# Summing the second MLP product over groups in DRAM instead of in on-chip tiles

## The chip, the cores and the metric

The kernel runs on one core of a Trainium2 chip. The metric is the time of one execution on the device in microseconds (us). Before the change three runs gave 1573.42, 1578.68 and 1580.87 us, so the median is 1578.68 us. One execution was recorded by the hardware profiler; its time and its trace are described below.

## What is computed

The reference is a two-layer block on 512 tokens of x and 256 tokens of a context, with 1024 features. Both streams share all weights. Each layer does, in this order:

- a modulated RMS norm, then a projection `zx = hx @ w_in`;
- token mixers on the projected features: an mLSTM in both directions, a Fourier mixer and a depthwise convolution, joined by `@ w_out`;
- a residual step with a norm and a gate;
- a second modulated norm, then the MLP, again followed by a norm, a gate and a residual step.

In layer 1 the context's output is not needed, so only the 512 tokens of x go through the projections after the keys and values. The part that the change touches is the MLP:

```
def sq_relu_mlp(h, w1, w2):
    return jnp.square(jax.nn.relu(h @ w1)) @ w2

hx = modulate(rmsnorm(x, g_pre_mlp[l]), mx[3], mx[4])
x = x + mx[5] * rmsnorm(sq_relu_mlp(hx, w_mlp1[l], w_mlp2[l]), g_post_mlp[l])
```

`w_mlp1` is 1024 x 4096 and `w_mlp2` is 4096 x 1024. All values are 32-bit floats.

## The kernel before

**Tiles.** Tokens are cut into six blocks of 128 (two of context, four of x). Every matrix is split into a high part and a low part, and a product is three matmuls: high times high, high times low and low times high. A weight tile is loaded as raw 32-bit numbers by a DMA that SP issues (L213), ScalarE (ACT) copies it to the high part (L219), and VectorE (DVE) subtracts to get the low part (L220). The function `prep` does this, `weight` hands out a finished pair, and calls `prep` for weights up to two ahead in a fixed list called `stream`.

**The MLP.** The 4096 hidden features are taken in eight groups `g` of 512, each of four tiles `f` of 128. For a group the first product gives the squared hidden values `gt[f]` (a high and a low tile each), and the second product, `mlp2` (L1025), multiplies them with the group's four weight tiles. Group 0 uses the plain first product. Groups 1 to 7 use `mlp1_pair`, a generator that makes two hidden tiles with seven half-size products (L1094) instead of eight; a group runs two such generators, `one_` and `two_`, interleaved by `next` calls. Between their steps stand calls of `background()`, which in layer 0 also work on the modulation of layer 1 (loads at L338, DVE products at L342).

In `mlp1_pair` the products of a late stage are accumulated on top of a PSUM bank `X` that ACT has to copy out first (L1118, L1124), so TensorE (PE) waits for that copy.

**The second product before.** For each half `hf` of the 1024 output columns and each block `b`, twelve matmuls fill one PSUM bank. In group 0 ACT copies the bank to the tile `acc[b]`, in groups 1 to 6 DVE adds it to `acc[b]`, and in group 7 it is added and the post-norm, gate and residual follow:

```
if g == 0:
    S.activation(ac_, ps, AF.Copy)
else:
    V.tensor_tensor(ac_, ps, ac_, ALU.add)
```

**Buffers.** `t4` is a pool of 8 tiles of 128 x 1024, `raw` one of 3 such tiles, `whi` has 6 and `wlo` 5 slots for the split weights, `mm` and `aux` are 4 PSUM banks each. In layer 0 the six `acc` tiles and, as long as the modulation of layer 1 runs, two more tiles (`box["c"]`) fill all of `t4`; in layer 1 it is four `acc` tiles. The raw weights of the MLP, the other weights and the background's loads share the three `raw` slots.

**What sets the order.** The instructions are written in program order, and a planner then lays out one fixed order for each engine from modelled durations: at every point it takes the ready instruction that stands first in program order, so a matmul of a later step may go ahead of an earlier one that is planned to wait. Slots of a pool are given out in program order. On the chip each engine and each DMA queue then keeps its order, and an instruction at its head that waits holds up what stands behind it.

Of the kernel before, what the change touches and what calls it, by code (L numbers as in the profile page):

```python
# [10 lines left out]
F32 = mybir.dt.float32  # L11
F32R = mybir.dt.float32r
AF = mybir.ActivationFunctionType
# [51 lines left out]
def build(tc, a):  # L65
# [20 lines left out]
    def nm(s):  # L86
        n_names[0] += 1
        return f"{s}{n_names[0]}"
# [59 lines left out]
    xd = [drp.tile([128, D], F32, name=f"xd{b}") for b in range(NB)]  # L148
    gd = [[drp.tile([2, D], F32, name=f"gd{l}_{g}") for g in range(2)] for l in range(DEPTH)]
    cd = drp.tile([2, D], F32, name="cd")  # L150
    md = [drp.tile([8, TOK], F32, name=f"md{l}") for l in range(DEPTH)]


# [31 lines left out]
    def prep(n):  # L185
        while st["next"] < min(n, len(stream)):
            key, src, (p, q) = stream[st["next"]]
            st["next"] += 1
            hi = hip.tile([128, 1024], F32R, tag="hi", name=nm("hi"))
            lo = lop.tile([128, 1024], F32R, tag="lo", name=nm("lo"))  # L190
            n_ = p * q
            parts = [t[:, :n_].rearrange("p (k n) -> p k n", k=p) for t in (hi, lo)]
            ready[key] = parts
            if key[0] == "dft":
                for i in range(2):
                    P.dma_start(parts[i], src[i])
                continue
            r0, n0 = 0, n_
            if key[0] in ("wt1", "wt2"):
                r1, r2 = pairs[key[1:]]  # L200
                if key[0] == "wt1":
                    raw = r2
                    V.tensor_tensor(r2[:, 0:512], r2[:, 0:512], r1[:, 0:512], ALU.subtract)
                    V.tensor_tensor(r2[:, 512:1024], r2[:, 512:1024], r2[:, 0:512], ALU.subtract)
                else:
                    raw = r1
                    V.tensor_tensor(r1.rearrange("p (k n) -> p k n", k=2), r1.rearrange("p (k n) -> p k n", k=2),
                                    r2[:, 512:1024].unsqueeze(1).to_broadcast([128, 2, 512]), ALU.subtract)
            elif key in pre:
                raw = pre.pop(key)  # L210
            else:
                raw = rawp.tile([128, 1024], F32, tag="raw", name=nm("raw"))
                dma(raw[:, :n_].rearrange("p (k n) -> p k n", k=p), src)  # L213
                if key[0] in ("wb1", "wb2"):
                    pairs.setdefault(key[1:], []).append(raw)
                    if key[0] == "wb2":

                        r0 = 512
            S.activation(hi[:, r0:n0], raw[:, r0:n0], AF.Copy)  # L219
            V.tensor_tensor(lo[:, r0:n0], raw[:, r0:n0], hi[:, r0:n0].bitcast(F32), ALU.subtract)  # L220
# [247 lines left out]
    def layer(l, res, nbg, first=None):  # L468
# [539 lines left out]
        yield "normed", None  # L1008


        acc = {}

        def mlp1_out(o, t0, n, th, tl):
            r = c2()
            S.activation(r[:, :n], o[:, :n], AF.Relu)
            V.tensor_tensor(r[:, :n], r[:, :n], r[:, :n], ALU.mult)
            split(r[:, :n], th[:, t0:t0 + n], tl[:, t0:t0 + n], True)

        def mlp2(ps, b, gt, ws, c0=0, c1=512):
            n = 0  # L1020
            for f in range(4):
                hi, lo = ws[f // 2]
                th, tl = gt[f]
                for hp, wp in ((th, hi), (th, lo), (tl, hi)):
                    T.matmul(ps, hp[:, 128 * b:128 * b + 128], wp[:, f % 2, c0:c1], start=n == 0, stop=n == 11)  # L1025
                    n += 1

# [106 lines left out]
        between = []  # L1136
        for g in range(NF // 4):
            gt = [(t3(F32R), t3(F32R)) for f in range(4)]
            if g == 0:

                w1 = [weight("w1", l, f) for f in range(4)]
# [7 lines left out]
            else:  # L1149
# [7 lines left out]
                background()  # L1157
                next(two_)
                background()
                for _ in two_:  # L1160
                    pass
                background()
            if g < NF // 4 - 1:
                for hf in range(2):
                    ws = [weight("w2", l, 4 * g + 2 * hf + i) for i in range(2)]
                    for b in oblk:
                        if b not in acc:
                            acc[b] = t4()
                        ps = mm()
                        mlp2(ps, b, gt, ws)  # L1170
                        ac_ = acc[b][:, 512 * hf:512 * hf + 512]
                        if g == 0:
                            S.activation(ac_, ps, AF.Copy)
                            if between:
                                between.pop(0)()
                        else:
                            V.tensor_tensor(ac_, ps, ac_, ALU.add)  # L1177
                continue
            G = {v: gate_row(l, 1, v) for v in ((0,) if last else (1, 0))}
            ws = [[weight("w2", l, 4 * g + 2 * hf + i) for i in range(2)] for hf in range(2)]  # L1180
            for b in oblk:
                o = acc[b]
                xr = [t3(), t3()]
                for hf in range(2):
                    dma(xr[hf][:, :512], xd[b][:, 512 * hf:512 * hf + 512])
# [1 line left out]
                cuts = (0, 256, 512, 768, 1024) if last and b == NB - 1 else (0, 512, 1024)  # L1187
                ms = None
                for i, (c0, c1) in enumerate(zip(cuts, cuts[1:])):
                    ps = mm()[:, :c1 - c0]  # L1190
                    h0 = 512 * (c0 // 512)
                    mlp2(ps, b, gt, ws[c0 // 512], c0 - h0, c1 - h0)
                    ac_ = o[:, c0:c1]
                    V.tensor_tensor(ac_, ps, ac_, ALU.add)
                    ss = ty(1, f"fs{i}")
# [213 lines left out]
```

## Time and profile before

| | |
|---|---|
| median of 3 runs | 1578.68 us (1573.42 to 1580.87) |
| the profiled execution | 1575.05 us, its span 1573.0 us |
| instructions | 23268 |
| PE busy | 1502.8 us (96%), mean granted clock 0.991 |
| DVE, ACT, POOL busy | 1094.1, 755.6 and 95.8 us |
| DMA | 197.30 MB, mean 125 GB/s |
| MLP of layer 0, groups 1 to 7 | 474.2 to about 942 us of the span |
| MLP of layer 1, groups 1 to 7 | 1255.2 to about 1565 us of the span |

The span runs from the first to the last instruction; the execution's time is 2.05 us longer. POOL is GpSimd, PE is TensorE, PEld its weight loads, SP the engine whose queue issues most DMAs. A clock of 1.00 is the higher of TensorE's two levels, 2.4 GHz, and 0.5 is the lower one, 1.2 GHz. A bracket behind a row gives the time in which the engine did nothing just before it, and what ended that wait.

### The profile page before, as it was taken

The numbers are of one execution on the slowest core, as the hardware profiler recorded it, in microseconds if no ns is written. First come the engines' busy times: TensorE is split into PE (matmuls) and PEld (weight loads), VectorE is DVE, ScalarE is ACT, GpSimd is POOL, SyncE is SP. The second block draws the span as 40 slices with busy tenths as digits, with TensorE's granted clock in tenths as the row PEclk, the third lists the DMA queues.
The fourth block names the chain that finished last, engine by engine and source line by source line (L and its number), as shares of the span: only waits on it lengthen the run. The fifth ranks groups of instructions, "written<-read, shape, count | busy, mean of one in ns | idle before, by whom it ended". The sixth has DMA issues, their size and how long they took to land. (4 is left out here: it accounts for less than half of the span.)

```text
span 1573.0 us, 23268 instructions
## 1 busy us (share of the span) xinstructions
PE 1502.8 (96%) x8926; PEld 1308.6 (83%) x8926; DVE 1094.1 (70%) x2101; ACT 755.6 (48%) x1471; POOL 95.8 (6%) x233
## 2 busy tenths in 40 slices
PE   7889999999998999999999998999999999999997
PEld 5868888987888889797888978788888888888886
DVE  3449987855899776675755575799756976666665
ACT  4633244536645343342524575544437655555443
POOL 0001022101000000000000011111101000000000
PEclk9999999999999999999999999999999999999999
DMA  8545436523534352441523332322225133333223
GB/s 322 136 140 191 158 109 209 194 73 134 181 102 137 105 188 89 139 151 64 187 68 107 103 134 101 122 80 80 83 81 174 55 120 98 104 108 96 94 81 119
DMA packets 65582, 197.30 MB, mean 125 GB/s; under 512 B 11904, under 2 KB 14368, under 8 KB 65472
## 3 DMA queue, kind: packets, MB, share of 16 engines
q1 hardware_dynamic: 64032, 191.10, 36.5%
q0 software_dynamic: 1440, 4.72, 0.9%
q8 instruction: 70, 1.15, 0.3%
q14 instruction: 40, 0.33, 0.1%
HBM read 183.13 MB, written 12.66 MB: 124 GB/s over the span
## 5 line engine op out<-in xcount | busy, mean ns | idle before, releaser
L219 ACT ACTIVATE hi<-raw 128x1024 fp32r<-128x1024 f32 (+1 forms) x245 | 244.6, 999 | 400.4 <-PE mm L1025 172.1
L1025 PE MATMUL mm<-hi,t 128*128 128x512 f32 (+1 forms) x1296 | 409.8, 394 | 6.8 <-ACT t L230 6.0
L220 DVE TENSOR_TENSOR lo<-raw,hi 128x1024 fp32r<-128x1024 f32 (+1 forms) x245 | 280.7, 1148 | 72.6 <-ACT hi L219 27.7
L1025 PEld LDWEIGHTS mm<-hi,t 128*128 128x128 f32 x1296 | 242.8, 189 | 65.7 <-ACT t L230 10.1
L1025 PE MATMUL mm<-lo,t 128*128 128x512 f32 (+1 forms) x648 | 253.5, 392 | 0.0
L457 PE MATMUL mm<-hhi,hi 128*128 128x256 f32 (+1 forms) x576 | 168.5, 336 | 0.0
L457 PE MATMUL mm<-hhi,lo 128*128 128x256 f32 (+1 forms) x576 | 166.5, 334 | 0.0
L457 PE MATMUL mm<-hlo,hi 128*128 128x256 f32 (+1 forms) x576 | 165.6, 332 | 0.0
L1177 DVE TENSOR_TENSOR t<-mm,t 128x512 f32<-128x512 f32 x120 | 82.3, 689 | 112.8 <-PE mm L1025 112.8
L1094 PE MATMUL mm<-hhi,hi 128*128 128x384 f32 (+1 forms) x448 | 141.0, 315 | 17.7 <-ACT c L1124 10.8
L1025 PEld LDWEIGHTS mm<-lo,t 128*128 128x128 f32 x648 | 122.5, 189 | 25.9
L1094 PE MATMUL mm<-hhi,lo 128*128 128x384 f32 (+1 forms) x448 | 139.1, 311 | 2.3 <-DVE lo L220 2.3
L1094 PE MATMUL mm<-hlo,hi 128*128 128x384 f32 (+1 forms) x448 | 139.0, 310 | 0.0
L457 PEld LDWEIGHTS mm<-hhi,hi 128*128 128x128 f32 x576 | 107.6, 189 | 15.5 <-issue 3.3
L457 PEld LDWEIGHTS mm<-hhi,lo 128*128 128x128 f32 x576 | 108.7, 189 | 12.1 <-issue 1.2
L457 PEld LDWEIGHTS mm<-hlo,hi 128*128 128x128 f32 x576 | 108.4, 189 | 10.9
L1094 PEld LDWEIGHTS mm<-hhi,hi 128*128 128x128 f32 x448 | 84.9, 190 | 25.3 <-ACT c L1124 15.7
L652 DVE SCALAR_TENSOR_TENSOR t<-t,half,t 128x783 f32<-128x783 f32 (+1 forms) x120 | 102.2, 888 | 0.3
L1094 PE MATMUL aux<-t,hi 128*128 128x384 f32 (+1 forms) x448 | 98.6, 310 | 0.2 <-DVE c L1125 0.2
L1094 PEld LDWEIGHTS mm<-hhi,lo 128*128 128x128 f32 x448 | 85.1, 190 | 2.6 <-DVE lo L220 2.6
L1094 PEld LDWEIGHTS mm<-hlo,hi 128*128 128x128 f32 x448 | 85.0, 190 | 0.7
L233 DVE TENSOR_TENSOR t<-c,t 128x256 fp32r<-128x256 f32 (+1 forms) x132 | 62.8, 478 | 24.6 <-ACT t L230 24.1
(244 smaller groups left out, 2729.8 us busy)
## 6 DMA issues: line engine op xcount, KB each, us to landing
raw<-w SPq DMA_DIRECT2D x128, 512.0 KB, 3.6
raw<-w_at SPq DMA_DIRECT2D x48, 512.0 KB, 3.5
raw<-w_a SPq DMA_DIRECT2D x44, 512.0 KB, 4.2
raw<-w_c SPq DMA_DIRECT2D x32, 512.0 KB, 5.1
xd<-t SPq DMA_DIRECT2D x20, 512.0 KB, 2.8
raw<-w_o SPq DMA_DIRECT2D x16, 512.0 KB, 3.6
t<-xd SPq DMA_DIRECT2D x20, 256.0 KB, 5.8
t<-x SPq DMA_DIRECT2D x8, 512.0 KB, 6.0
```

Source lines behind the costliest of these rows:

```text
L219: S.activation(hi[:, r0:n0], raw[:, r0:n0], AF.Copy)
L220: V.tensor_tensor(lo[:, r0:n0], raw[:, r0:n0], hi[:, r0:n0].bitcast(F32), ALU.subtract)
L233: V.tensor_tensor(blk_lo, src, blk_hi.bitcast(F32), ALU.subtract)
L457: T.matmul(o[:, :n], wp[:, k, :], hp[:, k, t0:t0 + n], start=k == 0 and i == 0, stop=k == KB - 1 and i == 2)
L652: V.scalar_tensor_tensor(o, u[j][:, o0 + k:o1 + k], w, o, ALU.mult, ALU.add)
L1025: T.matmul(ps, hp[:, 128 * b:128 * b + 128], wp[:, f % 2, c0:c1], start=n == 0, stop=n == 11)
L1094: T.matmul(ps[:, :HN], wp[:, K2 * j + k, :], hp, start=first and k == 0 and i == 0, stop=k == K2 - 1 and i == 2, skip_group_check=True)
L1177: V.tensor_tensor(ac_, ps, ac_, ALU.add)
```

## The change

Three things are changed together.

1. The tiles `acc` go. In groups 0 to 6 ACT copies each PSUM bank to a fresh `t4` tile. In group 0 a DMA of SP's queue writes it to a new DRAM tensor `ad[l][b]`; in groups 1 to 6 a DMA of POOL's queue adds it to what is there (`accum_op=ALU.add`). In group 7 the sum is loaded back to a `t4` tile and the rest goes on as before.
2. The raw weights of the MLP (`w1`, `w2`, `wb1`, `wb2`) are loaded to tiles of `t4` instead of `raw`.
3. In groups 1 to 7 the first two weight tiles of the second product are fetched before the last step of `two_`, and the matmuls of the first two blocks with `f` 0 and 1 are written there, into two PSUM banks that are finished later with `f` 2 and 3.

The diff, cut to its core:

```diff
+    ad = [[drp.tile([128, D], F32, name=f"ad{l}_{b}") for b in range(NB)] for l in range(DEPTH)]
 ...
-                raw = rawp.tile([128, 1024], F32, tag="raw", name=nm("raw"))
+                mlp = key[0] in ("wb1", "wb2", "w1", "w2")
+                raw = t4() if mlp else rawp.tile([128, 1024], F32, tag="raw", name=nm("raw"))
 ...
-        def mlp2(ps, b, gt, ws, c0=0, c1=512):
-            n = 0
-            for f in range(4):
+        def mlp2(ps, b, gt, ws, c0=0, c1=512, fs=range(4)):
+            for f in fs:
                 hi, lo = ws[f // 2]
                 th, tl = gt[f]
-                for hp, wp in ((th, hi), (th, lo), (tl, hi)):
-                    T.matmul(ps, hp[:, 128 * b:128 * b + 128], wp[:, f % 2, c0:c1], start=n == 0, stop=n == 11)
-                    n += 1
+                for n, (hp, wp) in enumerate(((th, hi), (th, lo), (tl, hi))):
+                    T.matmul(ps, hp[:, 128 * b:128 * b + 128], wp[:, f % 2, c0:c1], start=f == 0 and n == 0,
+                             stop=f == 3 and n == 2)
 ...
                 next(two_)
                 background()
+                ws0 = [weight("w2", l, 4 * g + i) for i in range(2)]
+                for b in oblk[:2]:
+                    early[b] = mm()
+                    mlp2(early[b], b, gt, ws0, fs=(0, 1))
                 for _ in two_:
                     pass
 ...
                     for b in oblk:
-                        if b not in acc:
-                            acc[b] = t4()
-                        ps = mm()
-                        mlp2(ps, b, gt, ws)
-                        ac_ = acc[b][:, 512 * hf:512 * hf + 512]
+                        if hf == 0 and b in early:
+                            ps = early[b]
+                            mlp2(ps, b, gt, ws, fs=(2, 3))
+                        else:
+                            ps = mm()
+                            mlp2(ps, b, gt, ws)
+                        o = t4()[:, 0:512]
+                        S.activation(o, ps, AF.Copy)
+                        to = ad[l][b][:, 512 * hf:512 * hf + 512]
                         if g == 0:
-                            S.activation(ac_, ps, AF.Copy)
+                            dma(to, o)
 ...
                         else:
-                            V.tensor_tensor(ac_, ps, ac_, ALU.add)
+                            P.dma_start(to, o, accum_op=ALU.add)
 ...
-                o = acc[b]
+                o = t4()
+                dma(o, ad[l][b])
```

## Rows read from the trace of the kernel before

**Rows 1.** Page, part 1: busy us, share of the span and instructions of each engine.

```profile
PE 1502.8 (96%) x8926; PEld 1308.6 (83%) x8926; DVE 1094.1 (70%) x2101; ACT 755.6 (48%) x1471; POOL 95.8 (6%) x233
```

**Rows 2.** Windows, layer 0's MLP groups: stretch, length, busy per engine, PEclk, DMA share, GB/s.

```profile
542.90:609.80 66.90, 64.80 (x313) 57.49 (x312) 43.80 (x81) 26.13 (x42) 0.00 (x0) 0.97 0.39 127
...
676.50:743.10 66.60, 64.49 (x314) 57.21 (x313) 42.99 (x76) 25.86 (x42) 0.00 (x0) 0.97 0.37 119
...
810.20:874.10 63.90, 63.49 (x315) 56.02 (x314) 37.99 (x62) 25.91 (x42) 0.00 (x0) 1.00 0.31 100
...
sum 424.90, PE 408.57 PEld 363.74 DVE 284.71 ACT 175.36 POOL 0.00; mean PE 58.37 PEld 51.96 DVE 40.67 ACT 25.05 POOL 0.00
```

**Rows 3.** Windows, layer 1's seven MLP groups up to 1542.9 us: their sum.

```profile
sum 287.70, PE 276.88 PEld 247.82 DVE 191.59 ACT 151.25 POOL 0.00; mean PE 39.55 PEld 35.40 DVE 27.37 ACT 21.61 POOL 0.00
```

**Rows 4.** Waits, layer 0's MLP (474 to 905): total us, times, longest us.

```profile
PE mm L1094 <- ACT c L1118: 6.9, 4, 2.0
PE mm L1025 <- ACT t L230: 6.0, 4, 2.1
PE mm L1094 <- DVE lo L220: 2.4, 2, 2.3
...
ACT hi L219 <- DMA raw<-w: 22.3, 20, 3.9
```

**Rows 5.** Waits of PE, ACT and SP's queue, layer 1's MLP (1255 to 1545).

```profile
PE mm L1094 <- ACT c L1124: 10.8, 7, 2.0
...
ACT hi L219 <- DMA raw<-w: 10.2, 11, 1.6
...
SPq L213 <- DVE lo L220: 246.6, 49, 13.0
```

**Rows 6.** Timeline, layer 1, group 1 before `two_`'s last step: start, us, engine, instruction.

```profile
1272.54 0.40 PE L1025 MATMUL mm<-hi,t 128*128 128x512 f32 x1
...
1273.80 1.06 ACT L219 ACTIVATE hi<-raw 128x1024 fp32r<-128x1024 f32 x1 [1.19 <-DMA raw<-w]
...
1275.18 0.40 PE L1094 MATMUL mm<-hhi,hi 128*128 128x256 f32 x1 [1.32 <-ACT c L1124]
```

**Rows 7.** Timeline, layer 0, group 3 after `two_`'s last step.

```profile
642.17 1.06 ACT L219 ACTIVATE hi<-raw 128x1024 fp32r<-128x1024 f32 x1 [1.05 <-DMA raw<-w]
...
648.12 0.50 PE L1025 MATMUL mm<-hi,t 128*128 128x512 f32 x1 [2.10 <-ACT t L230]
```

**Rows 8.** Groups of instructions: count, busy us, mean ns, idle before.

```profile
L1177 DVE TENSOR_TENSOR t<-mm,t 128x512 f32<-128x512 f32 x120 | 82.3, 689 | 112.8 <-PE mm L1025 112.8
...
L1173 ACT ACTIVATE t<-mm 128x512 f32<-128x512 f32 x20 | 11.7, 587 | 3.1 <-PE mm L1025 3.0
```

**Rows 9.** Timeline, DVE, one addition between two blocks of the second product.

```profile
721.14 0.69 DVE L1177 TENSOR_TENSOR t<-mm,t 128x512 f32<-128x512 f32 x1 [2.08 <-PE mm L1025]
```

**Rows 10.** POOL's table loads: duration ns min/median/max, and time to landing.

```profile
L196 POOL DMA_DIRECT2D hi<-dft_x x4: 546/570/595, 255.7 to 1102.6; - x4
...
DMA to landing us min/median/max: 3.6/5.2/8.3
```

**Rows 11.** DMA issues: queue, count, KB each, median us to landing.

```profile
raw<-w SPq DMA_DIRECT2D x128, 512.0 KB, 3.6
...
out<-t SPq DMA_DIRECT2D x8, 256.0 KB, 2.0
```

**Rows 12.** Windows, ten us in which only the second product runs, layer 0.

```profile
584.00:594.00 10.00, 10.00 (x45) 8.11 (x44) 4.97 (x8) 0.70 (x1) 0.00 (x0) 1.00 0.02 10
```

**Rows 13.** Timeline, end of layer 0's last group: ACT, PE, POOL.

```profile
918.23 1.06 ACT L402 ACTIVATE t<-t 128x1024 f32<-128x1024 f32 x1 [0.43 <-DVE t L1198]
...
922.06 1.09 PE L417 MATMUL aux<-ident_sb,t 128*128 128x128 f32 x8 [1.20 <-ACT t L404]
...
944.89 0.55 POOL L396 TENSOR_TENSOR fr<-fs1m,nhalf 128x1 f32<-128x1 f32 x1 [3.75 <-ACT fs1m L391]
...
957.31 2.64 POOL L396 TENSOR_TENSOR pr<-prm,nhalf 128x1 f32<-128x1 f32 x1 [3.48 <-ACT prm L391]
```

More of the change, by code (lines that the diff above doesn't have):

```diff
@@ L1008, in layer @@
         yield "normed", None
-        acc = {}
         def mlp1_out(o, t0, n, th, tl):
@@ L1138, in layer @@
             gt = [(t3(F32R), t3(F32R)) for f in range(4)]
+            ws0, early = None, {}
             if g == 0:
@@ L1164, in layer @@
                 for hf in range(2):
-                    ws = [weight("w2", l, 4 * g + 2 * hf + i) for i in range(2)]
+                    ws = ws0 if ws0 and hf == 0 else [weight("w2", l, 4 * g + 2 * hf + i) for i in range(2)]
                     for b in oblk:
-                        if b not in acc:
-                            acc[b] = t4()
-                        ps = mm()
-                        mlp2(ps, b, gt, ws)
-                        ac_ = acc[b][:, 512 * hf:512 * hf + 512]
+                        if hf == 0 and b in early:
[7 more added lines that the diff above has]
+                        to = ad[l][b][:, 512 * hf:512 * hf + 512]
                         if g == 0:
-                            S.activation(ac_, ps, AF.Copy)
+                            dma(to, o)
                             if between:
@@ L1176, in layer @@
                         else:
-                            V.tensor_tensor(ac_, ps, ac_, ALU.add)
+                            P.dma_start(to, o, accum_op=ALU.add)
                 continue
             G = {v: gate_row(l, 1, v) for v in ((0,) if last else (1, 0))}
-            ws = [[weight("w2", l, 4 * g + 2 * hf + i) for i in range(2)] for hf in range(2)]
+            ws = [ws0] + [[weight("w2", l, 4 * g + 2 + i) for i in range(2)]]
             for b in oblk:
-                o = acc[b]
+                o = t4()
+                dma(o, ad[l][b])
                 xr = [t3(), t3()]
@@ L1189, in layer @@
                 for i, (c0, c1) in enumerate(zip(cuts, cuts[1:])):
-                    ps = mm()[:, :c1 - c0]
                     h0 = 512 * (c0 // 512)
-                    mlp2(ps, b, gt, ws[c0 // 512], c0 - h0, c1 - h0)
+                    if c0 == 0 and b in early:
+                        ps = early[b][:, :c1 - c0]
+                        mlp2(ps, b, gt, ws[0], c0 - h0, c1 - h0, (2, 3))
+                    else:
+                        ps = mm()[:, :c1 - c0]
+                        mlp2(ps, b, gt, ws[c0 // 512], c0 - h0, c1 - h0)
                     ac_ = o[:, c0:c1]
```

## The prediction

> **What bounds the kernel now.** I read the busy times first. TensorE is busy for 1502.8 of 1573.0 us [rows 1], the other engines for 70% or less. So time can only be won where PE stands still or runs slowly, and no part of this change takes a matmul away. Next I cut the MLP into its groups. In layer 0, groups 1 to 7 take 424.9 us to the end of their first products and PE is busy for 408.57 of them: 16.3 us are idle [rows 2]. In layer 1 it is 287.7 against 276.88: 10.8 us idle [rows 3]. Group 6 of layer 0, nearly without idle time, takes 63.9 us with 63.49 of PE; groups 2 and 4 show 64.80 and 64.49 of PE at a mean granted clock of 0.97 [rows 2], so two short falls to the lower level cost 1.3 and 1.0 us, 2.3 together. These 29.4 us are all that the MLP's middle can give back.
>
> Then I asked the waits what stands behind the idle time. In layer 1 it is one thing, seven times: the last step of the second generator waits for ACT's copy L1124, 10.8 us in all [rows 5]. The timeline shows why. PE has run six matmuls of the second product (1272.54 + 6 x 0.23 = 1273.9) and stops until 1275.18. ACT's copy is late because the weight copy L219 in front of it stood 1.19 us for a raw load [rows 6]. The load is late because its issue waits for a `raw` slot: SP's queue waits 246.6 us, 49 times, for the subtraction L220 that frees one [rows 5], while a load lands 3.6 us after its issue [rows 11]. In layer 0 the idle time is mixed: 6.9 us for L1118, 6.0 us for the split of the hidden values L230, 2.4 us for L220 [rows 4]. ACT waits there for raw loads too, 22.3 us, 20 times [rows 4], and of the 2.10 us that PE lost at 648.12 a wait of 1.05 us for a load is directly ahead [rows 7]; the rest is work of ACT and of the background.
>
> **The change part by part.**
>
> Raw weights in `t4`: in layer 1 eight slots instead of three take the raw tiles and the partial sums, in layer 0 six (two hold the background's tiles), and the background has the three `raw` slots to itself. A load then leaves SP some microseconds earlier, and the waits of 1.0 to 1.6 us that delay L1124 go. No instruction is added.
>
> First blocks early: no matmul is added, twelve matmuls of 0.231 us are written before the last step of `two_`, 2.77 us. The planner already moves six of them there in layer 1 [rows 6]; six more are 1.39 us of cover against gaps of 1.3 to 2.0 us. Both edits work on the same seven gaps. I take 9.5 of the 10.8 us as gone; bounds 0 (the planner shifts the wait) and 10.8. In layer 0 I take half of the 16.3 us, 8, because about half of the idle time that I followed has a load ahead of it; bounds 0 and 16.3. Of the clock's 2.3 us I take half, 1.2, as the falls lie beside gaps; bounds 0 and 2.3.
>
> What is late next: after the last step the first blocks need `f` 3, whose values are made last. PE covered that with matmuls of which six more are now spent: at most 1.39 us per group, 13 groups, 18 us. The other two PSUM banks allow two further blocks with three of four `f`, 2 x 9 x 0.231 = 4.2 us of other cover, so I take a loss of 2; bounds 0 and 18.
>
> Sums in DRAM: DVE loses 120 additions of 0.689 us, 82 us; ACT gets 120 copies of 0.587 us, 70 us [rows 8]. A block takes 0.69 + 2.08 = 2.77 us of PE [rows 9], so one copy per block fits. ACT, now busy for 175 of 425 us and 151 of 288 us [rows 2, 3], comes to 217 (72 x 0.587 more) and 179: not a bound. DVE's relief buys nothing by itself, it isn't the bound. Cost 0; if ACT's order puts a copy behind a late load, PE has three further PSUM banks, 8.3 us, before it feels it. POOL issues 120 accumulating DMAs. POOL's issue of a table load takes 0.57 us [rows 10]: 68 us in stretches where POOL is at 0.00 [rows 2, 3], and nothing else is queued behind on POOL until the next norm's power. The trace has no accumulating DMA. Its landing time lies between 2.0 us (a plain 256 KB store, [rows 11]) and, going by twice the slowest load of POOL's queue for reading and writing, 16.6 us (2 x 8.3, [rows 10]). I take 5.2, the median of that queue, the nearest row. A slot of `t4` is then held for 0.59 + 0.57 + 5.2 = 6.4 us, 2.3 blocks, and the slots last. DMA engines have room: in the middle of the second product they are at 0.02 of their time [rows 12].
>
> The Trainium skill ("SBUF — State Buffer", the note on the trap "DVE blocks DMA") says that descriptors of a DMA issued by GpSimd are written by GpSimd itself, which is locked out while VectorE runs an operation that takes the port pair they share. The trace shows a stretch of that kind for POOL's arithmetic, 2.64 us where another takes 0.55, beside a busy DVE [rows 13]; it shows none for a DMA issue, 0.546 to 0.595 us [rows 10]. By the rule the slot life grows by some 2.1 us, to 8.5, which leaves the sum as it is and makes rival C below likelier.
>
> Group 0 and group 7: 20 stores and 10 loads on SP's queue, each needed long after its issue: 0, at worst a late load of 3.6 us at a layer's end. In layer 0's last group the six `acc` and two gate tiles filled `t4`, so the first block's norm could only start when block 1 had freed a gate tile (it waits for L1198 at 918.23), and PE idled 1.20 us at 922.06 [rows 13]. That wait goes: 1.2 (0 to 1.2).
>
> **Sum:** 9.5 + 8 + 1.2 + 1.2 - 2 = 17.9 us. The profiled execution took 1575.05 us, 2.05 more than its span; less 17.9 that is 1557. The median of the runs, 1578.68, is 3.6 above it, so I predict 1561 for the median.
>
> **The rivals.**
>
> *A, the forecast*, 1561: chance 0.58.
>
> *B, the gap only moves.* The six further matmuls are missing behind the last step, where the hidden values' chain through ACT and DVE sets the pace. For it: in layer 0 this is already the place of 6.0 us [rows 4]. Against: more PSUM banks' worth of other matmuls. Price: up to 18 us back, so 1578.7 - 19.9 + 18 = about 1577. Chance 0.20, no change that can be measured (this kernel's runs tell 0.5%, 7.9 us, from nothing).
>
> *C, the accumulating DMA holds the tiles.* In layer 0 six slots serve sums and weights; if weights hold two, four blocks, 4 x 2.77 = 11.1 us, is the longest life of a sum's slot. It decides from a landing of 11.1 - 1.16 = 9.9 us on. Then ACT's copy waits for a slot, with the weight copies behind it, and PE runs out of PSUM. At a landing of 12 us a block takes (12 + 1.16) / 4 = 3.29 us, 0.52 more, times 72 blocks: 37 us lost in layer 0, while layer 1 with six slots (2.19 per block) keeps its gain of 9.5. That is 1578.7 + 37 - 9.5 = 1606. For it: no row shows such a DMA and 8.3 us has occurred. Against: a median of 5.2, and idle DMA engines. Chance 0.16. (By the Trainium skill's rule above the point falls to 7.8 us, below the slowest row, and C would get 0.22.)
>
> *D, everything goes.* All 29.4 and 1.2, no loss: 1578.7 - 30.6 = 1548. Chance 0.06.
>
> **How the numbers follow.** Faster by over 0.5%, below 1570.8, are A and D: 0.64. Within 0.5% is B: 0.20. Slower is C: 0.16. The range reaches down to D with 2 us for the scatter of the runs, 1546, and up into C's milder part, 1590 (a landing of about 11 us); about 0.04 lies below and 0.12 above. A's own range is 1552 to 1570.
>
> **What would show it.** Right: in layer 1 the seven waits for L1124 are gone or below 0.3 us each; ACT's waits for raw loads in the MLP fall from 32 us to under 10; PE idle in the MLP's middle falls from 27 to about 10 us; the accumulating DMAs land in 4 to 7 us; the wait of PE for L230 does not exceed 8 us. B: that wait grows to 20 us or more. C: ACT's copies wait for a DMA of the partial sums, and PE for ACT's copies, in layer 0 above all. Also wrong would be a gain that shows outside the MLP.

## The result and the profile after

The changed kernel takes 1592.04 us (median of six runs, 1589.42 to 1598.54) against 1579.75 us for the kernel before in the same comparison: ratio 1.0088, 95% interval 1.0063 to 1.0114. It is slower by about 0.9%; the forecast was 1561 us. The profiled execution took 1592.11 us with a span of 1590.4 us, 17.4 us more than before.

The page of the changed kernel, parts 1, 3, 5 and 6 (an issue row is: queue, count, KB each, median us to landing):

```profile
PE 1507.0 (95%) x8926; PEld 1312.4 (83%) x8926; DVE 1011.6 (64%) x1981; ACT 818.8 (51%) x1591; POOL 194.7 (12%) x353
...
q1 hardware_dynamic: 68352, 201.59, 37.0%
q0 software_dynamic: 18720, 36.18, 14.0%
...
L1187 POOL DMA_DIRECT2D ad<-t x120 | 103.4, 899 | 680.2 <-ACT t L1180 680.0
...
t<-w SPq DMA_DIRECT2D x128, 512.0 KB, 5.3
ad<-t POOLq DMA_DIRECT2D x120, 256.0 KB, 5.6
raw<-w_at SPq DMA_DIRECT2D x48, 512.0 KB, 4.5
```

With as many matmuls as in [rows 1] PE is busy for 4 us more, at a mean granted clock of 0.982 against 0.991, and stands still for 13 us more. DVE lost the 82 us of its additions, ACT gained 63 where 70 were worked out. Raw weights of the MLP now land 5.3 us after their issue instead of 3.6 [rows 11].

Line numbers have moved by three up to the MLP: L213, L219, L220, L230, L338 and L342 of the kernel before are L216, L222, L223, L233, L341 and L345 here. L1180 is ACT's copy of a partial sum, L1187 POOL's accumulating DMA, L1209 DVE's addition in group 7.

Windows, layer 0's groups 1 to 4 of the changed kernel and the sum of groups 1 to 6 (columns as in [rows 2]):

```profile
480.90:548.60 67.70, 64.85 (x313) 57.13 (x311) 51.79 (x118) 32.63 (x53) 6.99 (x8) 0.97 0.65 190
548.60:627.00 78.40, 65.54 (x313) 58.21 (x313) 54.90 (x138) 30.56 (x53) 11.27 (x13) 0.93 0.84 254
627.00:701.60 74.60, 65.73 (x314) 58.40 (x313) 35.37 (x59) 35.39 (x58) 12.03 (x14) 0.93 0.63 155
701.60:764.50 62.90, 62.90 (x315) 56.12 (x314) 25.49 (x33) 32.41 (x54) 10.28 (x12) 1.00 0.52 115
...
sum 409.20, PE 384.62 PEld 342.07 DVE 218.36 ACT 195.80 POOL 61.19; mean PE 64.10 PEld 57.01 DVE 36.39 ACT 32.63 POOL 10.20
```

Groups 4 to 6 run without a gap, in 62.9 us, which no group of [rows 2] does. Groups 2 and 3 take 78.4 and 74.6, with 13 and 9 us of idle PE and a granted clock of 0.93. What differs between them is DVE's work: 55 and 35 us where groups 4 to 6 have 25. The surplus is the background, the modulation of layer 1.

Layer 1's groups 1 to 6 (the sum in [rows 3] is over seven groups):

```profile
1284.10:1326.60 42.50, 42.48 (x266) 37.64 (x266) 26.85 (x37) 27.95 (x53) 6.11 (x7) 1.00 0.62 166
...
sum 255.30, PE 255.22 PEld 225.39 DVE 142.68 ACT 157.47 POOL 40.52; mean PE 42.54 PEld 37.57 DVE 23.78 ACT 26.25 POOL 6.75
```

Here the forecast came true: 0.1 us of idle time is left in six groups, and PE's waits for L1124 [rows 5] are gone.

### The profile page after: what moved, and what is told of

It reads as the page before. It is cut to its first block, busy times and chain, and to the rows that moved or that the text cites. A ratio compares the mean times of both kernels' runs of the same rounds, so it can differ in the third digit from the quotient of the medians.

```text
span 1590.4 us, 23709 instructions
## 1 busy us (share of the span) xinstructions
PE 1507.0 (95%) x8926; PEld 1312.4 (83%) x8926; DVE 1011.6 (64%) x1981; ACT 818.8 (51%) x1591; POOL 194.7 (12%) x353
## 5 line engine op out<-in xcount | busy, mean ns | idle before, releaser
L223 DVE TENSOR_TENSOR lo<-t,hi 128x1024 fp32r<-128x1024 f32 (+2 forms) x187 | 211.6, 1134 | 178.4 <-ACT hi L222 138.5
L222 ACT ACTIVATE hi<-t 128x1024 fp32r<-128x1024 f32 (+2 forms) x187 | 182.5, 986 | 84.4 <-DMA t<-w 42.2
L1187 POOL DMA_DIRECT2D ad<-t x120 | 103.4, 899 | 680.2 <-ACT t L1180 680.0
L1180 ACT ACTIVATE t<-mm 128x512 f32<-128x512 f32 x140 | 82.9, 596 | 150.5 <-PE mm L1025 131.0
L460 PEld LDWEIGHTS mm<-hhi,lo 128*128 128x128 f32 x576 | 109.6, 191 | 13.3 <-DVE lo L223 1.5
L222 ACT ACTIVATE hi<-raw 128x1024 fp32r<-128x1024 f32 (+2 forms) x61 | 62.1, 1019 | 111.9 <-PE mm L460 48.2
L460 PEld LDWEIGHTS mm<-hlo,hi 128*128 128x128 f32 x576 | 109.8, 191 | 11.0 <-DVE hlo L236 0.2
## 6 DMA issues: line engine op xcount, KB each, us to landing
ad<-t POOLq DMA_DIRECT2D x120, 256.0 KB, 5.6
ad<-t SPq DMA_DIRECT2D x20, 256.0 KB, 2.0
```

Source lines behind the costliest of these rows:

```text
L460: T.matmul(o[:, :n], wp[:, k, :], hp[:, k, t0:t0 + n], start=k == 0 and i == 0, stop=k == KB - 1 and i == 2)
L1180: S.activation(o, ps, AF.Copy)
L1187: P.dma_start(to, o, accum_op=ALU.add)
```

## The experiments

Two theories stood at the start. **T1**: buffers are given in program order, so loads that now take `t4` tiles wait for what stands ahead of them there. **T2**: layer 1's modulation, with three buffers for itself, loads in a burst, and with the accumulates fills the DMA engines. Later ones, as they are named in the expectations: **T4**, six tiles are too few; **T2a**, bytes; **T2b**, the place of the `w_at` loads in the fixed queue.

To compare kernels I cut the span of the profiled execution at PE's first matmul of each stage: the first `w_o` product, the first `mlp1_pair` product of group 1, that of group 7, the next layer's `w_o`, and so on to the last matmul. "Step" is from `w_o` to group 1, "1-6" the six groups, "7" the last group and what follows it. Each ratio is to runs of the kernel before on the same chip (their medians were 1575.4 to 1579.8).

| kernel | median us | ratio to before [95%] | start | step, l0 | 1-6, l0 | 7, l0 | step, l1 | 1-6, l1 | 7, l1 |
|---|---|---|---|---|---|---|---|---|---|
| before | | 1 | 330.2 | 144.0 | 399.9 | 285.3 | 95.8 | 263.4 | 45.9 |
| after | 1592.0 | 1.0088 [1.0063, 1.0114] | 332.2 | 148.7 | 409.2 | 291.7 | 102.3 | 255.3 | 42.6 |
| e1_raw_rawp | 1585.5 | 1.0044 [1.0028, 1.0061] | 330.4 | 143.5 | 406.0 | 293.0 | 96.1 | 259.4 | 45.2 |
| e2_last_only | 1572.3 | 0.9972 [0.9957, 0.9987] | 329.9 | 143.3 | 402.0 | 287.0 | 102.8 | 255.1 | 42.6 |
| e3_early_only | 1571.3 | 0.9956 [0.9942, 0.9971] | 334.1 | 143.3 | 402.6 | 282.9 | 95.8 | 258.4 | 42.9 |
| e4_ad_ahead | 1581.9 | 1.0026 [1.0010, 1.0042] | 328.8 | 148.9 | 409.8 | 283.7 | 103.1 | 255.0 | 42.6 |
| e5_plain_store | 1580.9 | 1.0033 [1.0018, 1.0049] | 329.2 | 148.9 | 394.8 | 294.2 | 103.1 | 255.2 | 42.5 |
| e6_wat_eighth | 1573.4 | 0.9979 [0.9964, 0.9994] | 331.7 | 149.8 | 388.7 | 292.3 | 102.4 | 255.2 | 42.6 |
| e7_before_eighth | 1562.0 | 0.9920 [0.9900, 0.9940] | 328.7 | 143.1 | 388.6 | 283.8 | 95.8 | 266.1 | 46.5 |
| e8_w1_rawp | 1579.9 | 1.0027 [1.0007, 1.0048] | 329.1 | 143.8 | 410.5 | 296.8 | 96.0 | 255.2 | 42.6 |
| e10_wat_one_tile | 1609.8 | 1.0220 [1.0196, 1.0243] | 330.0 | 150.3 | 421.6 | 297.6 | 102.4 | 256.1 | 42.6 |
| e11_hold_two | 1593.2 | 1.0108 [1.0071, 1.0144] | 329.2 | 149.0 | 407.8 | 295.8 | 103.1 | 254.7 | 42.5 |
| e12_no_row_tiles | 1595.9 | 1.0127 [1.0100, 1.0155] | 329.5 | 150.4 | 407.7 | 296.6 | 102.9 | 256.0 | 42.6 |
| e13_w1_and_ad | 1568.9 | 0.9949 [0.9931, 0.9967] | 331.4 | 143.0 | 409.8 | 283.4 | 95.9 | 255.1 | 42.6 |
| e14_last_only_w1 | 1564.5 | 0.9936 [0.9908, 0.9964] | 331.2 | 143.6 | 401.3 | 285.1 | 95.9 | 255.2 | 42.6 |
| e15_wat_pool_queue | 1595.7 | 1.0115 [1.0089, 1.0141] | 331.8 | 148.7 | 410.3 | 296.5 | 102.9 | 255.1 | 42.6 |
| e16_one_tile_eighth | 1589.6 | 1.0070 [1.0043, 1.0097] | 331.0 | 148.9 | 405.4 | 297.8 | 103.0 | 255.1 | 42.6 |
| e17_wat_act_queue | 1592.3 | 1.0100 [1.0073, 1.0126] | 331.9 | 149.2 | 407.3 | 294.4 | 102.5 | 255.1 | 42.6 |
| e18_wat_t4 | 1542.8 | 0.9784 [0.9759, 0.9809] | 330.1 | 142.9 | 383.5 | 282.5 | 95.9 | 255.1 | 42.6 |
| e20_wat_t4_no_early | 1547.1 | 0.9802 [0.9779, 0.9826] | 332.4 | 143.2 | 383.8 | 283.3 | 96.2 | 256.0 | 42.7 |

Before to after reads +2.0 (start), +4.7, +9.3, +6.4, +6.5, -8.1, -3.3: +17.5 us. The start is scatter: it lies between 328.7 and 334.1 in kernels that do the same there. The last group scatters too: where it is as in the changed kernel, it and what follows take 291.7 to 297.8 us. Losses sit in three places: the step into the MLP (twice), layer 0's groups 2 and 3, and layer 0's last group. Groups 2 and 3 lose 19.4 us against the kernel before; groups 1 and 4 to 6 win about 10 of them back.

### The step into the MLP

In the planner's fixed order of SP's queue, one letter per DMA (`o` a `w_o` load, `1` and `2` raw weights of the first and second product, `x` a store of a block's row, `a` a `w_at` load, `S` a store of a partial sum, `.` another), this stretch reads

```
before  o.oooo1111x.x.x.x.2x.2ax..
after   o1o1.oooaaax.x.x.x.x.x1122..
```

Two of the four `w1` loads stand behind all row stores, because their buffers come from `t4`, which gives them in program order, behind the tiles of every block of the `w_o` stage. Timeline and window of the changed kernel:

```profile
413.75 1.46 PE L420 MATMUL aux<-ident_sb,t 128*128 128x128 f32 x8 [2.07 <-ACT t L407]
416.94 0.58 PE L460 MATMUL mm<-hhi,hi 128*128 128x256 f32 x1 [1.74 <-ACT hi L222]
```

```profile
413.70:420.00 6.30, 4.05 (x18) 3.36 (x19) 4.44 (x8) 5.56 (x11) 0.00 (x0) 0.55 1.01 369
```

The granted clock is near the lower level in this stretch (0.55); in the same 6.3 us of the span of the kernel before it was 1.00, with 5.83 us of busy PE. `e8_w1_rawp` undoes just this:

```diff
-mlp = key[0] in ("wb1", "wb2", "w1", "w2")
+mlp = key[0] in ("wb1", "wb2", "w2")
```

> The changed kernel; only group 0's first-product weights (w1) go back to the pool of three, all other raw weights of the MLP stay in the common pool. T1 (order of the buffers at the stage before the MLP): the step from w_o to group 1 falls from 148.7 to 144 us in layer 0 and from 102.5 to 96 in layer 1, the rest stays: 1591 less 11, 1580 us (1577 to 1584). If the longer step comes of the w2 tiles or of the norm's own chain, no change: 1591.

The steps fell to 143.8 and 96.0 us, as in the kernel before; 1579.9 us. So the place of the `w1` tiles is what made the steps longer.

### The last group of layer 0

```profile
935.36 1.29 DVE L1209 TENSOR_TENSOR t<-mm,t 128x512 f32<-128x512 f32 x2 [4.44 <-DMA t<-ad]
```

```profile
967.67 0.59 PE L507 MATMUL mm<-hi,hhi 128*128 128x264 f32 x1 [5.40 <-DVE t L1209]
```

DVE waits for the sum that comes back from DRAM, and PE for DVE. `e4_ad_ahead` asks for the next block's tile before the row store and the next norm:

```diff
-    o = t4()
-    dma(o, ad[l][b])
+    sum_of(b)                   # t4() and the load, once per block
+    o = got[b]
...
+    sum_of(b + 1)
     dma(xd[b], o)
     yield "next", (o, b)
```

> The changed kernel; in the last group of each layer the tile of the next block's sum is asked for, and its load issued, before the store of this block's row and the next layer's norm of it, instead of behind them. T1 (buffers in program order): in layer 0's last group VectorE's wait for the load of ad (4.44 us at 935.36) and TensorE's gaps of 2.8, 1.4, 5.4 us behind L1209 mostly go: -5 us, 1587 (1585 to 1590). The rival, that these gaps come of VectorE's and ScalarE's longer chain in the last group and not of the load: no change, 1592.

The stage fell by 8.0 us to 283.7, under the kernel before; more than expected. The two repairs together:

> Two mended steps together, each of which took 9 to 10 us off the changed kernel alone: w1 back in the pool of three, and the sums of the next block asked for ahead of the store. They lie in different stages (w_o to group 1 of both layers; the last group of layer 0), so they add: 1590 less 19, 1571 us (1568 to 1575), some 0.3% under the kernel before.

1568.9 us: they add, and the kernel is now faster than before by 0.5% [0.3, 0.7]. Layer 0's groups are untouched (409.8).

### Which part brings layer 1's gain

`e1_raw_rawp` gives the raw weights their pool of three back:

```diff
-mlp = key[0] in ("wb1", "wb2", "w1", "w2")
+mlp = False
```

> The changed kernel with one part undone: the raw weights of the MLP go back to their own pool of three, sums in DRAM and early blocks stay. Two theories for the loss (1592.0 against 1579.8). T1, slots: a pool gives its buffers in program order, so a raw weight in the common pool cannot be asked for before the tiles that stand ahead of it in the program, at the w_o stage those of the last block, in layer 0's groups the 256 KB halves whose buffers are free only when their accumulating DMA has landed. By T1 TensorE's gaps of 9.6 and 8.7 us in layer 0 (at 566.90 and 644.67) go, and so do the two extra gaps between w_o and MLP (4.7 us in layer 0, some 4 in layer 1); layer 1's waits of 10.8 us in the middle groups come back; the last group of layer 0 stays 5.8 us late. Sum 1592 - 11 - 9 + 10 = 1582 us (1577 to 1587). T2, bytes: the DMA engines are full because layer 1's w_at loads now have three buffers for themselves and run in a burst, while each accumulate holds the engines longer than a store. By T2 the two large gaps shrink too, since w_at must share its buffers again, but the gaps between w_o and MLP, where no w_at and no accumulate runs, stay: 1591 or so.

The steps went back, the two large gaps went, and 4.7 of layer 1's 11.4 us of gain stayed. But layer 0's groups took 406.0 us all the same, by many small waits of PE, all over the span:

```profile
PE mm L1025 <- ACT t L233: 16.5, 11, 3.0
PE mm L1094 <- ACT c L1118: 9.5, 9, 2.5
```

The first is the cover that the prediction saw lost behind the last step. `e3_early_only` is the kernel before with the early blocks alone, `e20_wat_t4_no_early` the fastest kernel (`e18_wat_t4`, below) without them. The edit of `e20`:

```diff
-    for b in oblk[:2]:
+    for b in ():
         early[b] = mm()
```

> The kernel before with the third part of the change alone: the first two blocks of the second product begun before the last step of the generator; accumulators in SBUF, VectorE's additions and the raw weights' pool as before. With sums in DRAM and this part (the first run) layer 1's groups took 43.2 us against 44.0 before and layer 0's 67.7 against 66.7. If the early blocks alone make the first and the sums in DRAM the second: layer 1 gains 0.8 a group, 5 us in all, layer 0 none: 1572 us (1568 to 1576). If the planner has already made this move, as the row at 1272 of the kernel before suggests, no change: 1577.

> The kernel of 1542.8 us (w_at's tiles from the common pool, w1 in its old pool, the next sum ahead) with no early blocks; everything else stays. If raw weights in time are enough for the waits behind L1124, layer 1's groups stay at 42.6 us and the time at 1543 (1539 to 1547). If the early blocks are what covers the copy, a gap of some 1 us comes back in each of 13 groups: 1556 us.

The early blocks alone give 8.0 us in layer 1 (258.4 + 42.9 against 263.4 + 45.9), nothing in layer 0, and 0.44% [0.29, 0.58] in time. With raw weights in time, leaving them out costs 1 us in layer 1 (`e20` against `e18`); at 1547.1 us `e20` is just above the range expected for it, and its ratio to the kernel before, 0.9802, agrees with `e18`'s 0.9784 within the intervals. Each of the two removes most of the same gaps; the prediction's "both edits work on the same seven gaps" holds.

`e2_last_only` keeps the whole change in layer 1 and none in layer 0, `e14_last_only_w1` puts `w1` back too:

```diff
+mlp = key[1] == DEPTH - 1 and key[0] in ("wb1", "wb2", "w2")   # e2: with "w1"
...
+if not last:                # layer 0: acc[b], as before
...
+        V.tensor_tensor(ac_, ps, ac_, ALU.add)
+    continue
```

> All three parts of the change in layer 1 alone; layer 0 keeps its accumulators in SBUF, VectorE's additions, the raw weights in their own pool and no early blocks, as before. If the gain in layer 1 is the change's own (11.5 us read between TensorE's stage bounds of the two traces) and all of the loss is in layer 0 and between w_o and MLP, the time is that of before less 11.5, plus some 4 us of the gap between w_o and MLP of layer 1, which this kernel keeps: 1572 us (1568 to 1576), under both kernels. If layer 1's gain was bought by something in layer 0 (w_at done earlier), it is near 1580.

> The run with the change in layer 1 alone came to 1572.3 us and still had the longer step from w_o to group 1 in layer 1 (102.8 us against 95.8 before). With w1 in the pool of three too that step goes back: 1572.3 less 6.5, 1566 us (1562 to 1569), 0.7% under the kernel before. If the step is not w1's, it stays at 1572.

Both came as expected, 1572.3 and 1564.5 us: layer 1's gain is its own, and the loss is in layer 0 and the steps.

### Layer 0's groups 1 to 3

The large gap of group 2 in the changed kernel, on PE, ACT and DVE, and SP's queue ahead of it:

```profile
566.90 0.69 PE L1094 MATMUL mm<-hhi,hi 128*128 128x384 f32 x1 [9.62 <-ACT c L1118]
```

```profile
564.08 1.06 ACT L222 ACTIVATE hi<-t 128x1024 fp32r<-128x1024 f32 x1 [12.39 <-DMA t<-w]
```

```profile
558.91 0.69 DVE L345 SCALAR_TENSOR_TENSOR raw<-raw,t 128x512 f32<-128x512 f32 x1 [4.65 <-DMA raw<-w_at]
```

```profile
541.24 12.23 SPq L341 DMA_DIRECT2D raw<-w_at  x4
553.57 10.69 SPq L216 DMA_DIRECT2D t<-w  x6
```

```profile
562.93 0.55 DVE L1113 TENSOR_TENSOR c<-mm,c 128x384 f32<-128x384 f32 x1
```

PE waits for ACT's copy L1118, which stands in ACT's order behind the weight copy L222, which waits 12.4 us for a raw weight. That load left SP late: for 12 us SP issued `w_at` loads, each waiting for one of its buffers, and then the weights' own tiles waited for accumulates. DVE is late as well: its L1113, which ACT's chain to L1118 needs, ran only at 562.93, behind the products L345 that waited for `w_at`, so it ended 0.6 us before the raw weight let ACT go. SP's waits from 480 to 700:

```profile
SPq L341 <- DVE raw L345: 90.0, 35, 9.5
SPq L216 <- DMA ad<-t: 36.0, 8, 13.0
```

The sum of such waits is not what sets the kernels apart: in the same window SP's `w_at` loads wait 115 us in all here (L341) and 98 in the kernel before (L338). What can differ is how many stand ahead of a raw weight.

So bytes, tiles or the place in the queues. First the bytes: an eighth of each `w_at` load, in the changed kernel and in the one before:

```diff
-dma(w, a["w_at"][l - 1, g, j, cb])
+dma(w[:, :, 0:64], a["w_at"][l - 1, g, j, cb][:, :, 0:64])
...                          # and the products read another operand
```

> The changed kernel with an eighth of the bytes of each w_at load (layer 1's conditioning weights, 48 loads of 512 KB in layer 0's MLP); VectorE's 60-odd products are as many and as long, but on another operand, so the conditioning of layer 1 is left out. Buffers, their order and all the accumulates are untouched. T1 (order of the buffers): the two gaps in layer 0 and those between w_o and MLP stay, 1590 us (1587 to 1593). T2 (DMA engines full of w_at and accumulates): loads and accumulates land in their unloaded time, the gaps of 9.6 and 8.7 us mostly go, 1581 (1577 to 1585).

> The control for the run with an eighth of w_at: the same cut in the kernel before. If the bytes of w_at cost the kernel before as much, the fall of 18 us says nothing of the change: 1560 us. By T2 the kernel before spreads these loads over all groups, since they share three buffers with the raw weights, and only part of its 16 us of idle time in layer 0's groups hangs on them: 1572 us (1567 to 1576).

1573.4 us, lower than either theory had, but the control fell as well, to 1562.0, by 11 us in the same groups. So a good part of the fall says nothing of the change, and my number for the control was wrong by 10 us. Like with like, the two kernels now spend the same in these groups (388.7 and 388.6 us): with an eighth of the bytes the 9.3 us of loss are gone, though in SP's queue the `w_at` loads still stand ahead in bursts of 11 and 18. One gap stays, in group 2, which takes 73.2 us. Plain stores in place of the accumulates:

```diff
-P.dma_start(to, o, accum_op=ALU.add)
+P.dma_start(to, o)
```

> The changed kernel with each accumulating DMA of POOL's queue made a plain store of the same 256 KB (so the sum over the groups is left out). Order, buffers and the w_at loads stay. The first four runs bear out that bytes in flight decide in layer 0: with an eighth of w_at the time fell by 18 us. T2 (w_at's burst and the accumulates fill the DMA engines together): a store holds the 16 engines for some 0.77 us instead of 1.74, so the 24 accumulates of groups 1 and 2 give back some 23 of 134 us of engine time; the gaps of 9.6 and 8.7 us shrink by half or more: 1591 less 12, 1579 us (1574 to 1584). If w_at's burst alone fills the engines, the accumulate being harmless: 1589 to 1592.

1580.9 us; the groups fell by 14 us to 394.8, below the 399.9 of the kernel before, and 69 and 71 us remain in groups 2 and 3. So slow transfers make the gaps longer, those of `w_at` and the accumulates both, but some of each gap is left without them.

One buffer for all `w_at` loads should have thinned the burst:

```diff
-w = rawp.tile([128, 2, 512], F32, tag="raw", name=nm("raw"))
+if "w" not in box:
+    box["w"] = rawp.tile([128, 2, 512], F32, tag="raw", name=nm("raw"))
+w = box["w"]
```

> The changed kernel with all bytes of w_at, but its loads go through one buffer, used again and again, so one load waits for the products of the one before: they take some 6.5 us each, 48 of them 310 us, to about 790 us of the span instead of 640. T2 (the burst): the two gaps in layer 0 go, as with an eighth of the bytes: 1591 less 18, 1573 us (1569 to 1578). If the bytes cost the same at any time, the gaps only spread over more groups: 1585 to 1591.

1609.8 us: worse, which neither account had. The gaps came in more groups (73 to 74 us in groups 3 to 5). Now an eighth of the bytes with that one buffer, and the two tests of the tiles:

> The run with one buffer for w_at, with an eighth of its bytes (layer 1's conditioning is left out). SP's queue still waits for that buffer at each load, some 2 us of landing and 1.4 to 2.8 us of products; the bytes are nearly gone. T2a (bytes): no gaps, 1573 us as with an eighth of the bytes and three buffers. T2b (SP's queue): the raw weights still wait behind the w_at loads, in more groups: 1585 us or above.

> The changed kernel; the two tiles of the common pool that the modulation of layer 1 holds in layer 0's MLP (box c) are kept until the last group by two copies of one column each, so six tiles instead of eight serve weights and sums in every group. w_at's loads still end near 640. T4 (six tiles are too few: a raw weight waits for the tile of a sum whose accumulate hasn't landed): groups 4 to 6, which run without a gap in 62.8 us each, go to 70 to 75 us, 1590 plus 20 to 36, so 1610 to 1626 us. T2 (w_at's traffic): groups 4 to 6 stay at 62.8, 1588 to 1592.

```diff
+for t in hold:                                # e11, in group 7 of layer 0
+    V.tensor_copy(ty(1, "hold"), t[:, 0:1])
...
-box["c"] = [t4() for _ in range(2)]           # e12; its products read w_at twice
```

> The mirror of the run that holds the two tiles: the changed kernel with all of w_at's bytes and as many products on VectorE, but on w_at itself, so that the two row tiles are never taken and eight tiles serve weights and sums from the first group (layer 1's conditioning is left out). T4: the gaps of 9.6 and 8.7 us go and groups 1 to 3 come to 63 to 65 us: 1590 less 20 to 28, about 1566 (1561 to 1571). T2 (traffic): the gaps stay, 1588 to 1592. If both are needed, in between.

Holding two tiles for the whole MLP left groups 4 to 6 at 63.1 us, and not taking them at all left groups 2 and 3 at 78.7 and 72.6. T4 is out: two tiles more or less decide nothing. `e16` with an eighth of the bytes of `w_at` still has 73.7, 72.0 and 70.2 us in groups 2 to 4, as T2b had it, so full bytes are not needed for a gap. DVE of that kernel, 480 to 700:

```profile
DVE raw L347 <- DMA raw<-w_at: 58.4, 17, 5.8
```

Then the queue alone, with all bytes:

```diff
-dma(w, a["w_at"][l - 1, g, j, cb])
+P.dma_start(w, a["w_at"][l - 1, g, j, cb])     # e17: S.dma_start
```

> The changed kernel; only the queue of the 48 w_at loads is another, POOL's instead of SP's. Bytes, buffers and products are the same. Open are two causes for the gaps of layer 0's groups 1 to 3. T2a, bytes: the DMA engines are full (share 0.89 to 1.05 where the sums are added). T2b, SP's queue: in its fixed order 10 to 18 w_at loads stand ahead of a group's raw weights, each waits for one of its three buffers, and the raw weights wait behind them. By T2a groups 1 to 3 stay at 67 to 78 us: 1588 to 1592. By T2b SP is free and the raw weights leave when their tiles are: groups 1 to 3 at 63 to 66 us: 1590 less 20, 1570 (1565 to 1578), unless the w_at loads now hold up the accumulates on POOL's queue, which would show as ACT's copies waiting for DMA ad.

> As the run with w_at on POOL's queue, but on ScalarE's. T2a: 1588 to 1592. T2b: SP is free, but a w_at load that waits for its buffer now holds up ScalarE's own copies behind it, up to 6 us at a time: somewhere between 1575 and 1595, with no wait of SP for raw buffers left and ScalarE's waits for DMA t<-w down from 41 us to below 20 in 540 to 700.

1595.7 and 1592.3 us, no gain, against my T2b. The Trainium skill ("DMA: Bandwidth & Descriptors", section "Issuing engines are not separate DMA queues") says that starting DMAs from several engines saves only the time of issuing. The times of these two runs do not speak against it, but they are no test of it, since another wait takes over. The waits of `e15` show where it stands now (PE from 475 to 700, the other engines from 480):

```profile
PE mm L1094 <- ACT c L1118: 23.5, 2, 13.6
```

```profile
ACT c L1099 <- DVE c L1113: 21.0, 4, 9.9
```

```profile
DVE raw L345 <- DMA raw<-w_at: 45.9, 18, 6.2
```

```profile
POOL raw L341 <- DVE raw L345: 124.6, 26, 41.2
```

SP is free of the background, but DVE is not. Its order still has the products of `w_at` ahead of the MLP's own work, it stops there for 45.9 us, and ACT and PE wait for DVE. The gap of group 2 is as long as before, since DVE's L1113 comes no earlier:

```profile
563.34 0.55 DVE L1113 TENSOR_TENSOR c<-mm,c 128x384 f32<-128x384 f32 x1
```

```profile
565.81 0.69 PE L1094 MATMUL mm<-hhi,hi 128*128 128x384 f32 x1 [9.91 <-ACT c L1118]
```

The raw weights came earlier here (ACT's waits for them fell from 41.5 to 12.8 us) although SP now waits 126.9 us for tiles of partial sums; ACT's copies wait 0.3 us for such a tile, so the risk that was named with this run is not what holds it. In the changed kernel DVE's row for `w_at` reads 35.2 us, in the kernel before 9.8:

```profile
DVE raw L345 <- DMA raw<-w_at: 35.2, 20, 4.7
```

```profile
DVE raw L342 <- DMA raw<-w_at: 9.8, 9, 1.6
```

So the background has to be moved back in every queue at once. `e18_wat_t4` takes `e13_w1_and_ad` and one edit:

```diff
-w = rawp.tile([128, 2, 512], F32, tag="raw", name=nm("raw"))
+w = t4().rearrange("p (i n) -> p i n", i=2)
```

> The kernel with w1 in the pool of three and the next block's sum ahead (1568.9 us), and w_at's loads take their tiles from the common pool too, on SP's queue, with all their bytes. Buffers are given in program order, so in SP's order 2 to 4 w_at loads stand between a group's raw weights, as before the change, instead of 10 to 18 ahead of them. T2b: layer 0's groups 1 to 6 fall from 409.8 to some 385 us: 1568.9 less 25, 1545 us (1540 to 1555). T2a: the bytes are spread over more groups, the gaps get smaller and more: 1565 to 1572.

1542.8 us, 2.16% [1.91, 2.41] under the kernel before and the fastest of all. SP's fixed order in groups 1 to 3 shows what the edit does:

```
before  aaaaaa221111aaaa22aaaa221111a.aa.22aaaa221111aaaa22aaaa
after   aaaaaaaSSSSS1S1SSSSS1S12222aaaaaaaaaa11aaaaa112222aaa.aaaaaaaaaaaaaaa11aaaaa.112222
e18     aaaaaaa22SSSSS1S1SSSSS1S1aaaa22aa22aa1111aaa22aa.22aa1111aaaa22aa22aa1111
```

With three buffers for itself the background is planned as early as buffers allow, 10 and 18 loads ahead of a group's first raw weights; sharing a pool with them, it is held to its place in the program. Windows of `e18_wat_t4`, layer 0, and its DVE wait:

```profile
473.00:542.40 69.40, 65.23 (x313) 57.55 (x312) 51.23 (x107) 35.23 (x57) 9.54 (x11) 0.98 0.65 175
542.40:605.20 62.80, 62.80 (x314) 56.15 (x314) 34.79 (x69) 32.15 (x54) 10.31 (x12) 1.00 0.72 180
605.20:668.00 62.80, 62.80 (x313) 56.07 (x312) 34.44 (x64) 32.16 (x54) 10.27 (x12) 1.00 0.73 184
...
sum 383.50, PE 379.33 PEld 338.21 DVE 217.99 ACT 195.38 POOL 60.95; mean PE 63.22 PEld 56.37 DVE 36.33 ACT 32.56 POOL 10.16
```

```profile
DVE t L345 <- DMA t<-w_at: 0.9, 1, 0.9
```

Groups 2 to 6 run gap-free at 62.8 us, with all bytes and fewer free tiles; SP's raw weights still wait 80.1 us for tiles of partial sums (480 to 700), more than the 36.0 of the changed kernel, and no gap comes of it. That DMA engines as full as 0.9 alone make no gap is seen in one stretch, 520 to 560, of the changed kernel and of `e18_wat_t4`: share 0.90 and 0.91, PE busy 36.57 and 40.00 of 40 us.

```profile
520.00:560.00 40.00, 36.57 (x168) 30.41 (x167) 20.79 (x53) 11.21 (x18) 10.49 (x12) 1.00 0.90 220
```

```profile
520.00:560.00 40.00, 40.00 (x199) 35.76 (x198) 19.39 (x36) 17.74 (x30) 8.01 (x10) 1.00 0.91 222
```

Shown: in the steps and in layer 0's last group it is T1 (`e8`, `e4`, `e13`). In layer 0's groups it is the place of the `w_at` work in the fixed orders, DVE's as well as SP's: `e18`, the one edit that restores the order, takes the six groups from 409.8 to 383.5 us with all bytes and removes the gaps of groups 2 and 3 (group 1, at 69.4 us, is no shorter). `e5` and `e6` show that the order costs what the transfers ahead take: shorter ones, still ahead, win back more than the 9.3 us. `e15` and `e17` show that freeing SP is not enough: in group 2's gap the raw weight and DVE's L1113 come 0.6 us apart, and with SP freed the gap is 9.91 us long. Left open: what DVE's order is worth alone, since no run moved it without SP's; and whether shorter accumulates help by the DMA engines or by tiles that come free earlier, since no run parts the two.

## Why the prediction was wrong

**The step that failed** is in the first part: "the background has the three `raw` slots to itself. A load then leaves SP some microseconds earlier". I booked it as a gain of 8 us for layer 0. Sharing three slots in program order was what held the background in its place; freed of it, the planner put 10 to 18 of the background's loads, and its products, ahead of a group's raw weights, and groups 1 to 6 of layer 0 lost 9.3 us against the kernel before, where `e18` gains 16.4. PE was idle for 24.6 us in these six groups alone, where about 10 us were forecast for the groups of both layers. Where the background's loads were done, in groups 4 to 6, the gain of that step did come: 9.2 us. Slots in program order and fixed queues, both told ahead of the prediction, could have shown it; I asked what the MLP gets, not what the other user of the pool will do.

**Costs left out.** The raw weights of group 0 went into a pool whose tiles are all in use at the `w_o` stage: 4.7 and 6.5 us in the two steps, which the sum doesn't have (`e8`). "20 stores and 10 loads on SP's queue, each needed long after its issue: 0" was wrong in layer 0: the load of a sum can't be issued long before, as its tile comes from the same pool: +6.4 instead of -1.2 (`e4` takes off 8.0).

**Terms that held.** Layer 1: 9.5 forecast, 11.4 measured (8.1 and 3.3), by the mechanism named. No loss behind the last step where raw weights are in time: PE's wait for L233 is 0.8 us in layer 0 after the change, where [rows 4] has 6.0 (predicted no more than 8); 2 us was booked. ACT's copies do not bound. ACT's waits for raw loads were to fall below 10 us: 0.7 in layer 1, but 41.5 in layer 0.

```profile
PE mm L1025 <- ACT t L233: 0.8, 1, 0.8
```

```profile
ACT hi L222 <- DMA t<-w: 41.5, 5, 12.4
```

**Sizes.** The accumulating DMA's issue on POOL, and its landing:

```profile
L1187 POOL DMA_DIRECT2D ad<-t x120: 845/857/1533, 522.8 to 1540.6; - x120
...
DMA to landing us min/median/max: 3.6/5.6/12.1
```

It lands in 5.6 us (5.2 taken), at worst in 12.1. POOL's issue takes 0.86 us, not 0.57. The 120 issues sum to 107.9 us (mean 899 ns; 103.4 us busy, as some overlap), 5 us more than 120 times the median, and the longest is 0.68 us above it; so the 2.1 us for each that the prediction worked out beside the Trainium skill's rule ("SBUF — State Buffer", the trap "DVE blocks DMA") are not seen here. The room on the DMA engines, 0.02 in [rows 12], was no measure of what was to come: 0.52 to 0.84 per group. The bound of 18 us behind the last step counts 13 groups; groups 1 to 7 of two layers are 14, 19.5 us, and nothing hangs on it.

**Rivals.** B did not happen. C had the right sign and place, but not the wait it named: ACT's copies waited once, 2.8 us, for a DMA of the partial sums in layer 0's groups, and `e11` and `e12` show that two tiles more or less change nothing. The length of the accumulates does count, as `e5` shows, where the order is wrong.

## What to carry to other kernels

When a tenant leaves a shared pool, ask what the others in it will now do earlier: with buffers given in program order, sharing is also what keeps a background job in its place in every engine's queue. Before a load's tile is taken from a pool of compute tiles, list what stands ahead of it in program order at that point, also in the stages next door. The wait that names a load on two engines at once (here SP and DVE at `w_at`) says where to look.

## What the runs showed of the hardware

By the time of its packets an accumulating DMA holds the DMA engines 2.6 times as long as a plain store of the same bytes from the same queue. The plain-store kernel's page:

```profile
q0 software_dynamic: 11040, 36.18, 6.0%
...
L1187 POOL DMA_DIRECT2D ad<-t x120 | 64.9, 542 | 704.8 <-ACT t L1180 703.3
...
ad<-t POOLq DMA_DIRECT2D x120, 256.0 KB, 2.9
```

The kernel before has 0.9% on that queue, 14.2 us of its span. So 120 stores take 0.060 x 1576.3 - 14.2 = 80 us of all 16 engines, 0.67 each; 120 accumulates 0.140 x 1590.4 - 14.2 = 208 us, 1.74 each. POOL's issue is 0.54 against 0.86 us, landing 2.9 against 5.6.

The two large gaps cost PE twice: behind the one of 9.62 us and the one of 8.70 (up to 644.67) it runs without a pause but at a granted clock of 0.78 and 0.76 for ten microseconds:

```profile
567.00:577.00 10.00, 10.00 (x46) 10.00 (x47) 9.96 (x23) 6.04 (x11) 0.00 (x0) 0.78 0.63 214
...
645.00:655.00 10.00, 10.00 (x46) 10.00 (x46) 6.13 (x8) 6.15 (x11) 0.00 (x0) 0.76 0.37 143
```

So groups 2 and 3 have 65.5 and 65.7 us of busy PE for the work that takes 62.9 in group 4.
